# An encoder layer on one core: differences of the weights tied to their place on DVE, bias tables copied in the value passes, masks between sums, turns of late tiles moved in two stages

## The chip, the cores and the metric

The kernel runs on 1 core of one Trainium2 chip. The metric is the device time of one execution in microseconds, the median of several runs. The engines are PE (TensorE, matmuls), PEld (its weight loads), DVE (VectorE), ACT (ScalarE), POOL (GpSimd) and SP, which here only issues DMAs.

## The reference, cut to what matters

```python
# x: (1, 1024, 1024) float32, one layer
h = swiglu(rmsnorm(x, ffn1_pre_g), w_gate1, w_up1, w_down1)      # D_FF = 2816
x = x + 0.5 * rmsnorm(h, ffn1_post_g)
h = rmsnorm(x, mix_pre_g)
q, k, v = split(h @ w_qkv)                                       # 16 heads of 64
o_na  = neighbourhood_attention(q[:8], k[:8], v[:8], na_rel_bias)   # 2-D window, bias, softmax
o_dil = dilated_mixture_attention(q[8:], k[8:], v[8:], t5_rel_bias) # 3 dilated windows, merged
x = x + rmsnorm(concat(rmsnorm(o_na), rmsnorm(o_dil)) @ w_out, mix_post_g)
h = swiglu(rmsnorm(x, ffn2_pre_g), w_gate2, w_up2, w_down2)
x = x + 0.5 * rmsnorm(h, ffn2_post_g)
```

All inputs and outputs are float32.

## The kernel before

**Numbers.** Every operand of a large matmul is split into two parts, `hi` (rounded by an ACT cast) and `lo` (the rest, one DVE subtraction), and a product is three matmuls, hi·hi, hi·lo and lo·hi (`mm3`, lines 317 to 319). Weights go through `split` (ACT line 413, DVE line 414) in the projections, and through `Passes.fetch` (ACT line 673, DVE line 674) in the passes below.

**Strassen's scheme.** The large products are cut into 2 by 2 blocks and done with seven products instead of eight (Winograd's form). On the side of the activations the sums are named A11, A12, A22, S1, S2, S3, S4, on the side of the weights B11, B21, B22, T1, T2, T3, T4, and the pairs are A11·B11, A12·B21, S2·T2, S1·T1, S4·B22, S3·T3, A22·T4. The rows of the activations are 8 tiles of 128. A11 and A12 need only tiles 0 to 3; the others need tiles 4 to 7 too, so those *late tiles* are normalized, transposed on PE and added up (`right_half`, lines 269 to 279) while PE already multiplies with A11 and A12.

**The stages, in order of time.**
- The opening and `PairGemm.ahead` of the first FFN (0 to 85 us): tiles 0 to 3 are normalized, then A11 and A12 products of 9 early blocks of the gate and up weights run while tiles 4 to 7 come in.
- `PairGemm.run` (85 to 470 us): per block five groups of 12 matmuls on PE. For an *early* block (the first 9 of 22; 10 of 22 in the second FFN, all 8 in the query and key projection) their order is S2·T2, then A22 of the block before (in `last`), S1·T1, S3·T1, S4·B22. A later block starts with A11, A22 of the block before, S2, A12, S1, S3, S4. `prepare(b + 1)` hands out the steps for the next block's weights: `direct` (for a later block the split `g`, then three subtractions, lines 502 to 504, which make T1, T2 and T4 from the raw block), `second` (T2's split), `sums` (T1's split) and `rest` (B22's split, and the loads of a raw block two further, lines 407 and 408). The result of S2 is added up in `u` (line 540), of S1 in `v` (line 548), of S3 in `c22` (line 567), of A22 in `c21` (line 575). For the gate, `last` ends with a SiLU on ACT (626) and line 627, and in every second block with four more DVE operations (635 to 638).
- `Passes` of the first FFN's down projection (470 to 689 us): seven passes, one for each product, `pw` split just ahead of use. In its turns `RightSums` makes T1 to T4 of the value weights (loads `tr`, three DVE subtractions at lines 385 to 387 tied behind DVE, one store `tsv`, then the load of the next into the same single buffer), and `masked` adds the mask to the bias tables of 8 heads (POOL line 875, loads and stores of `nb`).
- The value projection's first two passes (689 to 717 us), the query and key projection's `ahead` (717 to 768), the value projection's passes 2 to 6 (768 to 823), the query and key projection's `run` (823 to 950, line 502 among its DVE work). In the first two the late tiles get their residual added (`fin.rest`, line 788), are normalized (squares at line 150 on ACT, `rstd_of` at lines 131 to 143, scaling at line 204) and transposed (`put`).
- Attention (950 to 1200), the output projection, the second FFN (to 1926 us).

**The order.** PE follows the order of the program everywhere. On all other engines a planner puts the instructions in order beforehand, by its own costs and due times: it may put one that it takes to be ready ahead of others that stand earlier in the program. An engine then runs its list strictly in that order, so an instruction that waits holds everything behind it. In the very first stretch (`begin`) DVE and ACT are in the program's order too. `c.behind(f, E)` is the one tool against the planner: what `f` issues on engine `E` is put behind the last instruction that the program had issued on `E` before it.

**Turns.** `plan(n, {i: steps})` fills a list of turns; each unit of matmuls ends with `c.tick()`, which runs one turn. Steps that a turn leaves behind (`put` of a tile: two transposes; pending sums) are run one by one inside the matmul loops (`c.step`). `plan` first flushes what is still open. `spread(steps, 36)` lays a list evenly over 36 turns. In the tables of turns `F` normalizes tiles, `L` loads them, `U` transposes one, `A` adds the residual and normalizes.

**Bias tables.** `c.toeplitz` are eight copies in DRAM (`gab` from `tab`, line 852, POOL's queue, 511 KB each) that lay out the T5 bias for the dilated heads.

Of the kernel before, what the change touches and what calls it, by code (L numbers as in the profile page):

```python
# [391 lines left out]
class PairGemm:  # L392
# [134 lines left out]
    def run(self, final=None):  # L527

        c, nc, sp = self.c, self.c.nc, self.c.sp
        last = None  # L530
        for b in range(self.n):
            w, early = self.w.pop(b), b < self.early
            direct, second, sums, rest = self.prepare(b + 1)
            if early:
                s1 = sp.tile([P, T], F32, tag="s1", name="s1")
                nc.sync.dma_start(s1, self.kept[b])
                a = self.bank()
                self.mm(a, w[T2], 0, S2)
                u2 = sp.tile([P, T], F32, tag="u2", name="u2")
                nc.vector.tensor_add(u2, a, s1)  # L540
                if last:
                    last()
                direct()
                second()
                a = self.bank()
                self.mm(a, w[T1], 0, S1)
                v = sp.tile([P, T], F32, tag="v", name="v")
                nc.vector.tensor_add(v, a, u2)  # L548
            else:
                a = self.bank()  # L550
                self.mm(a, w["g"], 0, A11)
                s1 = self.keep(a, "s1")
                if last:
                    last()
                self.mm(a, w[T2], 0, S2, True)
                u2 = self.keep(a, "u2")
                pb = self.bank()
                self.mm(pb, w["g"], 1, A12)
                self.sink.first(b, pb, False, s1)
                direct()  # L560
                second()
                self.mm(a, w[T1], 0, S1, True)
                v = self.keep(a, "v")
            d = self.bank()
            self.mm(d, w[T1], 1, S3)
            c22 = c.cp.tile([P, T], F32, tag="g2", name="c22", bufs=3)
            nc.vector.tensor_add(c22, d, v)
            sums()
            self.mm(a, w[B22], 0, S4, True)
            self.sink.second(b, a, u2 if early else None)  # L570

            def last(b=b, d=d, w=w, u2=u2, c22=c22, rest=rest):
                self.mm(d, w[B22], 1, A22, True)
                c21 = c.cp.tile([P, T], F32, tag="c", name="c21")
                nc.vector.tensor_add(c21, d, u2)  # L575
                rest()
                self.sink.last(b, c21, c22)
            c.tick()
        if final:
            final()  # L580
        last()
# [657 lines left out]
def layer(tc, a, out):  # L1239
    nc = tc.nc  # L1240
    c = Ctx(tc)
    with ExitStack() as ctx:
# [50 lines left out]
        def plan(n, at):  # L1293

            c.flush()

            def turn(fs):
                return lambda: [f() for f in fs]
            c.todo.extend(turn(at.get(i, ())) for i in range(n))

        def spread(steps, n, skip=0):
            m, n = len(steps), n - skip
            plan(n + skip, {skip + k: steps[m * k // n:m * (k + 1) // n] for k in range(n)})
# [19 lines left out]
        def ffn(which, op, prep, pg, get, turns, sums, more, post, pre, src, dst, begin=None, tables=()):  # L1323
# [57 lines left out]
            ps.take = combine(c, fin.half, rows)  # L1381
            if masks:
                c.bp = pool("bp", 1, m)
            spread(more + masks, 36)
            c.todo[7] = lambda f=c.todo[7]: (f(), c.behind(
                lambda: nc.scalar.activation(fin.gain, fin.gain, AF.Copy, scale=0.5), ACT))
            ps.run(0, 1, 2, 3, 4)
# [61 lines left out]
        with ExitStack() as order:  # L1449
# [25 lines left out]
            def begin(pg):  # L1475
# [92 lines left out]
                for b in range(3):  # L1568
                    if b:
# [5 lines left out]
                order.close()  # L1575
                order.enter_context(ordered())
                return s1
            F = lambda *ts: lambda: op0.norm(ts, [xs[t] for t in ts])
            L, U = (lambda *ts: lambda: load(ts, [nc.gpsimd] * 2)), (lambda t: lambda: op0.put(t))
            op, fin, hs, prep = ffn(1, op0, prep, gate_pairs(1, op0, a["wg1"], a["wu1"], 9), get1,  # L1580
                                    {0: [F(4, 5), L(6, 7)], 1: [U(4)], 2: [F(6, 7), U(5)], 4: [U(6)], 5: [U(7)]},
                                    down_sums(a["wd1"], ts1), value_sums(a["wv"], tsv),
                                    a["ffn1_post_g"], a["mix_pre_g"], x0, x1, begin,
                                    bias_steps(c, *[a[k] for k in ("na_rel_bias", "t5_rel_bias", "onehot", "lncount", "cmask")]))
# [9 lines left out]
            def vearly(p, t, ps):  # L1594
# [4 lines left out]
                else:  # L1599
# [3 lines left out]
            pg = PairGemm(c, op, [(a["wqk"][p], a["wqk"][8 + p]) for p in QK_ORDER], 8, QKPairs(c))  # L1603
            p0 = pg.own = pool("p0", 1, prep, side="right")
            vp.fetch([[p0.tile([P, 2, T], F32R, tag="g" + h, name="pw0" + h) for h in ("hi", "lo")]])
            plan(12, {0: [lambda: fin.scale(4, 4), A(4, 5)], 4: [A(6, 7)], 7: [U(4)], 9: [U(5), lambda: queued(pg.start)],
                      11: [lambda: pg.split_left(0)]})
            vp.run(0, 1, upto=1)
            e.close()
            early_pools(e, 2, 2)  # L1610
            c.qkbufs = 2
            plan(8, {1: [U(6)], 3: [U(7)]})
            pg.ahead()
            c.flush()
            e.close()
# [8 lines left out]
                nc.gpsimd.dma_start(c.v[1][t * P:(t + 1) * P, :], h[:, 1])  # L1624
            vp.take = combine(c, lambda t, g, h: None, vrows)
            nc.sync.dma_start(c.second[:, :, 0], vs1.rearrange("t p x -> p t x"))
            vp.run(2, 3)
            pg.fetch(0)
            pg.fetch(1)
# [9 lines left out]
            def first_bias():  # L1639
                by_residue(nc.gpsimd.tensor_copy, loaded[0][2][:, 0], loaded[0][2][:, 2])  # L1640
            e1 = c.small.tile([P, 1], F32, tag="e1", name="e1", bufs=1)
            plan(8, {**{i: c.toeplitz[2 * i:2 * i + 2] for i in range(4)}, 5: [lambda: queued(load_head)], 7: [lambda: queued(load_head), lambda: queued(first_bias),
                     lambda: c.behind(lambda: nc.scalar.activation(e1, c.ident[:, :1], AF.Exp), ACT)]})
            pg.run()
            w.close()
# [204 lines left out]
```

## Time and profile before

| what | value |
|---|---|
| median of 3 runs | 1929.8 us (1928.88 to 1931.73) |
| the profiled execution | 1927.83 us, its span 1926.0 us |
| PE busy | 1851.6 us, 96% of the span |
| DVE busy | 1325.9 us, 69% |
| ACT busy | 832.0 us, 43% |
| POOL busy | 319.9 us, 17% |
| mean granted clock of PE | 0.988 |

Matmuls overlap each other, and their ends are modelled, so the busy time of PE says only where it had something in flight; what is left, 74.4 us, is time in which it had nothing. "A <- B" in a list of waits reads: the instruction group A waited until B ended; the numbers are the total in us, how often, and the longest. In a timeline a row has the start and the length in us, the engine, the line and the tiles, and in brackets the idle time before it with what ended it. In a table of stretches (windows) the columns are the length, the busy time and instruction count of PE, PEld, DVE, ACT and POOL, then the granted clock of PE, the busy share of the DMA engines, and GB/s. In a list of DMA issues the last number is the median time in us from issue to landing.

### The profile page before, as it was taken

The numbers are of one execution on the slowest core, as the hardware profiler recorded it, in microseconds if no ns is written. First come the engines' busy times: TensorE is split into PE (matmuls) and PEld (weight loads), VectorE is DVE, ScalarE is ACT, GpSimd is POOL, SyncE is SP. The second block draws the span as 40 slices with busy tenths as digits, with TensorE's granted clock in tenths as the row PEclk, the third lists the DMA queues.
The fourth block names the chain that finished last, engine by engine and source line by source line (L and its number), as shares of the span: only waits on it lengthen the run. The fifth ranks groups of instructions, "written<-read, shape, count | busy, mean of one in ns | idle before, by whom it ended". The sixth has DMA issues, their size and how long they took to land.

```text
span 1926.0 us, 25147 instructions
## 1 busy us (share of the span) xinstructions
PE 1851.6 (96%) x8904; PEld 1536.5 (80%) x8904; DVE 1325.9 (69%) x2233; ACT 832.0 (43%) x1491; POOL 319.9 (17%) x504
## 2 busy tenths in 40 slices
PE   7899999999999989998899998999999999999997
PEld 6787888888778867877799997877888888888886
DVE  6777776765565875556677765777788777654557
ACT  7422333333344555223488765455222333344332
POOL 2123211111030122122433100121111111110000
PEclk9999999999999999999999999999999999999999
DMA  7656565547886757556968540575456655476563
GB/s 270 211 169 207 204 225 211 195 164 248 295 306 216 269 187 257 193 178 221 299 224 259 170 142 23 190 280 186 158 192 238 216 193 210 159 267 216 200 227 136
DMA packets 169296, 404.95 MB, mean 210 GB/s; under 512 B 17793, under 2 KB 40225, under 8 KB 167122
## 3 DMA queue, kind: packets, MB, share of 16 engines
q1 hardware_dynamic: 121330, 242.66, 37.9%
q0 software_dynamic: 46832, 158.59, 22.9%
q10 hardware_dynamic: 1008, 2.10, 0.3%
q8 instruction: 70, 1.15, 0.2%
q14 instruction: 56, 0.46, 0.1%
HBM read 277.34 MB, written 130.99 MB: 212 GB/s over the span
## 4 chain that ended last, share of the span: by engine, by line
PE 47%; issue 27%; DMA 9%; DVE 9%; POOL 3%; ACT 3%; SPq 1%; DVEq 0%; POOLq 0%; ACTq 0%
PE mmp L319 9%; PE mmp L317 9%; PE mmp L318 9%; PE accp L318 4%; PE accp L319 4%; PE accp L317 4%; PE po L1072 2%; PE ptp L982 2%; DMA wraw<-in_wqk_dram 2%; PE po L1184 2%; DMA wraw<-in_wu_dram 1%; DVE pw L674 1%; DMA tsv<-tr 1%; PE sp L1051 1%; DVE wlo L414 1%
## 5 line engine op out<-in xcount | busy, mean ns | idle before, releaser
L317 PE MATMUL mmp<-x,whi 128*128 128x512 f32 (+1 forms) x1464 | 581.4, 397 | 19.4 <-DVE v L548 10.9
L319 PE MATMUL mmp<-x,wlo 128*128 128x512 f32 (+1 forms) x1464 | 577.5, 394 | 3.9 <-DVE wlo L414 3.9
L318 PE MATMUL mmp<-x,whi 128*128 128x512 f32 (+1 forms) x1464 | 575.7, 393 | 1.3 <-DVE x L240 0.8
L317 PEld LDWEIGHTS mmp<-x,whi 128*128 128x128 f32 x1464 | 278.2, 190 | 84.7 <-ACT whi L413 10.0
L319 PEld LDWEIGHTS mmp<-x,wlo 128*128 128x128 f32 x1464 | 277.9, 190 | 68.6 <-DVE wlo L414 5.9
L318 PEld LDWEIGHTS mmp<-x,whi 128*128 128x128 f32 x1464 | 278.3, 190 | 62.6 <-DVE x L240 1.1
L674 DVE TENSOR_TENSOR pw<-praw,pw 128x1024 fp32r<-128x1024 f32 (+1 forms) x181 | 199.7, 1148 | 115.7 <-ACT pw L673 115.3
L673 ACT CAST pw<-praw 128x1024 fp32r<-128x1024 f32 (+1 forms) x181 | 168.6, 982 | 208.3 <-PE accp L319 150.3
L318 PE MATMUL accp<-pw 128*128 128x512 f32 x600 | 234.4, 391 | 5.9 <-DVE pw L674 5.6
L317 PE MATMUL accp<-pw 128*128 128x512 f32 x600 | 234.8, 391 | 0.3 <-DVE hb L730 0.2
L319 PE MATMUL accp<-pw 128*128 128x512 f32 x600 | 233.6, 389 | 0.0
L413 ACT CAST whi<-wraw 128x1024 fp32r<-128x1024 f32 x129 | 135.3, 1051 | 219.1 <-PE mmp L318 184.5
L414 DVE TENSOR_TENSOR wlo<-wraw,whi 128x1024 fp32r<-128x1024 f32 x129 | 158.2, 1228 | 19.9 <-ACT whi L413 19.7
L318 PEld LDWEIGHTS accp<-pw 128*128 128x128 f32 x600 | 112.7, 188 | 31.6 <-DVE pw L674 9.0
L317 PEld LDWEIGHTS accp<-pw 128*128 128x128 f32 x600 | 112.7, 188 | 25.1 <-ACT pw L673 1.2
L319 PEld LDWEIGHTS accp<-pw 128*128 128x128 f32 x600 | 112.6, 188 | 23.3
L621 POOL DMA_DIRECT2D g<-sg x44 | 23.9, 544 | 471.1 <-DVE sg L614 296.4
L413 ACT CAST whi<-traw 128x512 fp32r<-128x512 f32 x52 | 32.4, 623 | 152.3 <-DVE traw L503 95.6
L502 DVE TENSOR_TENSOR wraw<-wraw 128x1024 f32<-128x1024 f32 x52 | 63.7, 1225 | 45.4 <-DMA wraw<-in_wqk_dram 26.2
L432 ACT COPY s<-mmp 128x512 f32<-128x512 f32 x52 | 30.6, 588 | 139.4 <-PE mmp L319 136.4
L575 DVE TENSOR_TENSOR c<-mmp,u 128x512 f32<-128x512 f32 x52 | 35.9, 690 | 76.9 <-PE mmp L319 76.8
L1184 PE MATMUL po<-vs,pt 128*128 128x128 f32 x352 | 50.3, 276 | 2.0 <-ACT pt L984 1.7
(278 smaller groups left out, 2761.1 us busy)
## 6 DMA issues: line engine op xcount, KB each, us to landing
praw<-g SPq DMA_DIRECT2D x70, 512.0 KB, 6.0
wraw<-in_wg_dram SPq DMA_DIRECT2D x44, 512.0 KB, 4.2
wraw<-in_wu_dram SPq DMA_DIRECT2D x44, 512.0 KB, 6.2
tr<-in_wd_dram SPq DMA_DIRECT2D x44, 512.0 KB, 6.5
g<-sg POOLq DMA_DIRECT2D x88, 256.0 KB, 4.1
ts<-tr POOLq DMA_DIRECT2D x22, 1024.0 KB, 4.8
praw<-ts SPq DMA_DIRECT2D x88, 256.0 KB, 4.3
praw<-in_wd_dram SPq DMA_DIRECT2D x66, 256.0 KB, 4.9
```

The source lines that it names most:

```text
L317: nc.tensor.matmul(out, ahi, bhi, start=start, stop=False, skip_group_check=go_on)
L318: nc.tensor.matmul(out, ahi, blo, start=False, stop=False, skip_group_check=go_on)
L319: nc.tensor.matmul(out, alo, bhi, start=False, stop=stop, skip_group_check=go_on)
L413: nc.scalar.copy(hi, raw)
L414: nc.vector.tensor_sub(lo, raw, hi.bitcast(F32))
L502: nc.vector.tensor_sub(r[:, 0:2], r[:, 1:3], r[:, 0:2])
L575: nc.vector.tensor_add(c21, d, u2)
L673: nc.scalar.copy(hi, raw[:, :m])
L674: nc.vector.tensor_sub(lo, raw[:, :m], hi.bitcast(F32))
L982: nc.tensor.transpose(ps[:, j, :], src[:, j * P:(j + 1) * P], c.ident)
L1072: nc.tensor.matmul(po[:, un * 2 + j], pt[:, 2 * j + t, :], rhs, start=t == 0, stop=t == 1)
L1184: nc.tensor.matmul(po[0][:, u], pt[0][:, j, :], vs[:, k0 + j, :], start=j == 0, stop=j == n - 1)
```

## The change

Five edits in one:
1. In `PairGemm.run`, `direct()` becomes `c.behind(direct, DVE)` for early and for later blocks: the DVE instructions of `direct` are put behind the last DVE instruction that the program issued before.
2. The nine mask steps no longer stand behind the five steps of the value weights' sums (one load, four sums), but two by two between them, over the same 36 turns.
3. In the opening the squares of `F` are put behind ACT's last instruction; tiles 6 and 7 are normalized at turn 1 instead of 2 and transposed at turns 5 and 6 instead of 4 and 5.
4. Around the value projection's first passes, `A(6, 7)` moves from turn 4 to turn 10, `U(4)` from 7 to 8, `pg.start` from 9 to 8, `split_left(0)` from 11 to 10, and `U(5)`, `U(6)`, `U(7)` go to turns 0, 3, 5 of the query and key projection's `ahead` (from turn 9 before it, and 1, 3 in it).
5. The eight copies of the bias table move from turns 0 to 3 of the query and key projection's `run` (two a turn) to every second turn, 0 to 14, of the value passes 2 to 6.

```diff
@@ PairGemm.run @@
                 if last:
                     last()
-                direct()
+                c.behind(direct, DVE)
                 second()
...
                 self.sink.first(b, pb, False, s1)
-                direct()
+                c.behind(direct, DVE)
                 second()
@@ ffn @@
-            spread(more + masks, 36)
+            steps = more[:1]
+            for i, f in enumerate(more[1:]):
+                steps += masks[2 * i:2 * i + 2] + [f]
+            spread(steps + masks[2 * len(more[1:]):], 36)
@@ layer, first FFN @@
-            F = lambda *ts: lambda: op0.norm(ts, [xs[t] for t in ts])
+            F = lambda *ts: lambda: c.behind(lambda: op0.norm(ts, [xs[t] for t in ts]), ACT)
...
-                                    {0: [F(4, 5), L(6, 7)], 1: [U(4)], 2: [F(6, 7), U(5)], 4: [U(6)], 5: [U(7)]},
+                                    {0: [F(4, 5), L(6, 7)], 1: [U(4), F(6, 7)], 2: [U(5)], 5: [U(6)], 6: [U(7)]},
@@ layer, value, query and key projection @@
-            plan(12, {0: [lambda: fin.scale(4, 4), A(4, 5)], 4: [A(6, 7)], 7: [U(4)], 9: [U(5), lambda: queued(pg.start)],
-                      11: [lambda: pg.split_left(0)]})
+            plan(12, {0: [lambda: fin.scale(4, 4), A(4, 5)], 8: [U(4), lambda: queued(pg.start)],
+                      10: [lambda: pg.split_left(0), A(6, 7)]})
...
-            plan(8, {1: [U(6)], 3: [U(7)]})
+            plan(8, {0: [U(5)], 3: [U(6)], 5: [U(7)]})
...
+            plan(20, {2 * i: [f] for i, f in enumerate(c.toeplitz)})
             vp.run(2, 3)
...
-            plan(8, {**{i: c.toeplitz[2 * i:2 * i + 2] for i in range(4)}, 5: [lambda: queued(load_head)], 7: [...
+            plan(8, {5: [lambda: queued(load_head)], 7: [...
```

More of the change, by code (lines that the diff above doesn't have):

```diff
@@ L1641, in layer @@
             e1 = c.small.tile([P, 1], F32, tag="e1", name="e1", bufs=1)
-            plan(8, {**{i: c.toeplitz[2 * i:2 * i + 2] for i in range(4)}, 5: [lambda: queued(load_head)], 7: [lambda: queued(load_head), lambda: queued(first_bias),
+            plan(8, {5: [lambda: queued(load_head)], 7: [lambda: queued(load_head), lambda: queued(first_bias),
                      lambda: c.behind(lambda: nc.scalar.activation(e1, c.ident[:, :1], AF.Exp), ACT)]})
```

## The prediction

> **What bounds the kernel now.** I read the page's first lines, then the list of waits of PE, then the granted clock and the DVE timeline of each place that the list names.
>
> ```profile
> span 1926.0 us, 25147 instructions
> PE 1851.6 (96%) x8904; PEld 1536.5 (80%) x8904; DVE 1325.9 (69%) x2233; ACT 832.0 (43%) x1491; POOL 319.9 (17%) x504
> ...
> PE mmp L317 <- DVE v L548: 10.9, 7, 2.8
> PE accp L318 <- DVE pw L674: 6.0, 7, 1.7
> PE trp L157 <- DVE x L204: 5.5, 1, 5.5
> PE trp L157 <- DVE xn L204: 4.9, 1, 4.9
> ...
> PE mmp L319 <- DVE wlo L414: 3.9, 3, 3.1
> ...
> PE mmp L317 <- ACT x L238: 2.6, 1, 2.6
> ```
>
> PE sets the end: 1926.0 - 1851.6 = 74.4 us are all that better timing alone can win there. The waits shown are 34 us of it, and all but the last are on DVE, which is busy only 69% of the span: what is wanted is done too late, not too slowly. Beside the waits stands the clock.
>
> ```profile
> 20.00:60.00 40.00, 31.02 (x149) 24.66 (x148) 32.43 (x64) 25.73 (x44) 11.88 (x22) 0.94 0.79 283
> 690.00:730.00 40.00, 31.38 (x131) 24.95 (x130) 30.69 (x66) 20.36 (x34) 11.17 (x20) 0.91 0.63 217
> 838.00:950.00 112.00, 98.85 (x429) 79.94 (x427) 71.57 (x96) 38.48 (x51) 32.41 (x46) 0.98 0.79 252
> 870.00:885.00 15.00, 12.59 (x50) 9.98 (x49) 11.67 (x15) 6.96 (x8) 5.37 (x8) 0.89 0.65 183
> 160.00:200.00 40.00, 39.80 (x172) 31.52 (x172) 31.33 (x43) 9.35 (x11) 12.28 (x22) 1.00 0.53 169
> ```
>
> What the column behind POOL's count (0.94, 0.91, 0.98) lacks of 1, times the length, is the clock lost in three stages: 2.4, 3.6 and 2.2 us. It goes where waits are, and is 1.00 in a gate stage without them (last row).
>
> **The change part by part.** The sum is made against the profiled execution (1927.8 us, span 1926.0 and 1.8 around it), which lies 2.0 under the median shown. An edit at a time:
>
> *D, the query and key run (edits 1 and 5).* Its order and its loads:
>
> ```profile
> PE mmp L317 <- DVE v L548: 10.7, 6, 2.8
> ...
> DVE wraw L502 <- DMA wraw<-in_wqk_dram: 24.4, 5, 6.6
> 851.46 1.23 DVE L502 TENSOR_TENSOR wraw<-wraw 128x1024 f32<-128x1024 f32 x1 [4.08 <-DMA wraw<-in_wqk_dram]
> 860.82 0.68 DVE L548 TENSOR_TENSOR v<-mmp,u 128x512 f32<-128x512 f32 x1
> 859.17 10.88 DMA wraw<-in_wqk_dram
> wraw<-in_wqk_dram SPq DMA_DIRECT2D x16, 512.0 KB, 6.3
> ```
>
> The planner has put `direct` (L502) ahead of `k` and `u`, although it stands behind `last` in the program. L502 waits for its raw block, DVE stands still (24.4 us in five blocks), everything behind it is late, and `v` holds PE: 10.7 of the 10.9 us lie between 838 and 950. Tied, `direct` comes behind `last`, where the block (it landed at 851.46, and is then wanted from about 859) is there; and without the copies, during which such loads take 10.88 us against a median of 6.3, it lands earlier. What is late next is T2 for the next S2. Behind the last line 931, `direct` to T2's `lo` takes 1.23 + 0.68 + 0.69 + 0.62 + 0.68 = 3.9 us (rows in E), while PE has S1, S3 and S4 to do, 8.2 us from the end of A22: nothing waits if line 931 ends within 4.3 us of it. An addition, three or four ACT operations and two subtractions of 0.6 to 1.1 us come first, some of them side by side, so I put it at 4.7: 0.4 us a block stay, 3 over eight. Gain 10.7 - 3 + 1.6 of the clock (870 to 885: 0.11 of 15) = 9, bounds 2 (`direct` only moved to another wait) and 12.9 (10.7 + 2.2).
>
> *E, the gate runs (edit 1).* PE does not wait there today, and this is the price. Rows of a block whose `last` ends with four more operations:
>
> ```profile
> 171.28 1.05 ACT L413 CAST whi<-wraw 128x1024 fp32r<-128x1024 f32 x1 [1.16 <-PE mmp L318]
> 169.50 0.62 ACT L413 CAST whi<-traw 128x512 fp32r<-128x512 f32 x1 [5.43 <-DVE traw L503]
> 166.96 1.23 DVE L502 TENSOR_TENSOR wraw<-wraw 128x1024 f32<-128x1024 f32 x1 [1.64 <-DMA wraw<-in_wu_dram]
> 171.11 0.68 DVE L414 TENSOR_TENSOR wlo<-traw,whi 128x512 fp32r<-128x512 f32 x1
> 176.88 0.69 DVE L638 TENSOR_TENSOR sg<-sg 128x512 f32<-128x512 f32 x1
> 850.53 0.39 PE L317 MATMUL mmp<-x,whi 128*128 128x512 f32 x1
> 853.25 0.39 PE L317 MATMUL mmp<-x,whi 128*128 128x512 f32 x1
> ```
>
> A group of 12 matmuls takes 853.25 - 850.53 = 2.72 us. The cast at 171.28 starts when A22 ends; S1, S3 and S4 follow, so the next S2 wants T2 at 171.28 + 8.2 = 179.4. Before, T2 was ready at 171.8, because `direct` had run at 167. Tied behind L638 (end 177.6), L502 and L503 (0.68, as line 414's half) end at 179.4, the cast at 180.1, T2's `lo` at 180.8, which S2's third matmul wants at 179.9: 0.7 to 0.9 us late, and 1.8 if T1's cast (1.05) goes first on ACT. I take 1.4. It hits blocks 3, 5, 7 of the first FFN and 3, 5, 7, 9 of the second: +10. In the other early blocks `direct` follows L627 and can push `v`, but by no more than one L502 of 1.23 less some 0.5 of slack: 0.7 each, of which I take nothing, as the planner would have to choose it. Later blocks start with A11 and A22, 5.4 us more: nothing; the S2 and A12 groups cover `direct` there. Bounds 0 (if the planner finds gaps for it) and 7 x 1.8 + 8 x 0.7 = 18.
>
> *A, the opening (edit 3).*
>
> ```profile
> 25.64 1.06 ACT L150 ACTIVATE xn<-x 128x1024 f32<-128x1024 f32 x1 [1.01 <-DMA x<-in_x_dram]
> 49.56 0.17 DVE L133 TENSOR_SCALAR v<-ss 128x2 f32<-128x2 f32 x1
> 56.58 2.48 DVE L204 SCALAR_TENSOR_TENSOR xn<-x,y,gain 128x1024 f32<-128x1024 f32 x2
> ```
>
> Two squares, for tiles 4 and 5, stand in front of the casts (L238) that PE waits for 2.6 us; the first waits 1.01 for its tile and takes 1.06. Behind ACT's last instruction they let the casts go some 1.9 us earlier, and tile 4, squared later, takes some of that back: 1.5. The wait of 4.9 us is tile 6: its chain of small operations runs from 49.56, between the sums of tile 5, to the scaling at 56.58; a turn sooner, it starts before these. A turn later is two groups, 5.4 us, which covers 4.9. But DVE is full there (32.43 of 40), so I take 4 of it. With 1 of the 2.4 us of clock: 1.5 + 4 + 1 = 6.5, bounds -2 (tile 7's sums, now in front of the last blocks' splits, hold one of them up by two operations of 0.69 and a little) and 10 (2.6 + 4.9 + 2.4).
>
> *B, sums and masks (edit 2).*
>
> ```profile
> DVE tr L385 <- DMA tr<-in_wv_dram: 20.2, 4, 7.3
> tr<-in_wv_dram SPq DMA_DIRECT2D x8, 512.0 KB, 4.5
> tsv<-tr POOLq DMA_DIRECT2D x4, 1024.0 KB, 8.1
> ```
>
> One round of the single buffer takes 4.5 + 8.1 + 2.6 (1.23 + 2 x 0.69) = 15 us. Four sums over turns 5 to 12 come faster and stop DVE for 20.2 us; PE loses most of its 6.0 us on `pw` behind them, and some of it because a load that waits for the buffer holds the `praw` loads behind it in SP's queue. With two masks between them they come every seven or eight turns, 16 to 20 us. The hold on SP's queue stays as long as it was; POOL, which adds the masks, is 17% busy and nobody in this stage waits for it. Gain 3, half, bounds -1 (masks and sums share the DMA engines) and 6.
>
> *C, late tiles around the value projection (edit 4).*
>
> ```profile
> 692.42 4.87 DVE L788 SCALAR_TENSOR_TENSOR x<-hb,y,x 128x1024 f32<-128x1024 f32 x4
> 702.55 2.48 DVE L204 SCALAR_TENSOR_TENSOR x<-x,y,gain 128x1024 f32<-128x1024 f32 x2
> 722.10 2.35 DVE L414 TENSOR_TENSOR wlo<-graw,whi 128x1024 fp32r<-128x1024 f32 x2
> ```
>
> PE waits 5.5 us for tile 4's scaling, which follows the residuals of four tiles and their squares. With tiles 6 and 7 at turn 10 half of the 4.87 us can come out from under it, of which I take 1.5, since the squares on ACT stay; and U(4) one turn later asks for it 2.7 later (one group): 1.3 of the wait stay, 4.2 go. The second wait, 3.1 us, is the split of the second weight block behind tile 5's sums; these go into the next stage, but tiles 6 and 7 bring 2 x 2.48 back. I take 1.3 of it, and 2 of the 3.6 us of clock: 7.5, bounds -3 (tile 7, two blocks later, late for S2) and 12.
>
> *F, eight copies in the value passes (edit 5).*
>
> ```profile
> DVE wraw L502 <- DMA wraw<-in_wqk_dram: 1.8, 2, 1.1
> ```
>
> These passes load four raw halves of the projection, and `begin`'s L502 stands for them in DVE's list ahead of `pw` splits. From the slow loads above (10.88 for 6.3) each may be up to 4.6 us later; PE has one or two splits in hand. I take +2, bounds 0 and 5. By the Trainium skill ("DMA: Bandwidth & Descriptors", Issuing engines are not separate DMA queues), DMAs of all engines share the same 16 DMA engines and interleave, so that POOL's copies only change whom they slow; by that rule F would be nearer +4.6 and the sum 2.6 less good. The trace agrees for the stage they leave (10.88); for the one they enter it shows nothing yet.
>
> Sum: -9 + 10 - 6.5 - 3 - 7.5 + 2 = **-14 us**. 1927.8 becomes 1913.8, and the median 1929.8 becomes 1916.
>
> **The rivals.**
> 1. *The ties cost nothing in the gates*, because T2's subtractions find DVE idle in the planner's list. For it: DVE idles before A22 ends (160 to 200: 31 of 40 busy). Against: L638's place. E = 0: -24, 1906.
> 2. *The waits only move.* DVE is as full around 50 and 700 as before, and the same work is late somewhere else. A -2, B -1, C -2, D -7, E +10, F +2 = 0: 1930. For it: 30.69 of 40 in C.
> 3. *Slower: T2 starves S2 in the gate runs.* 18 us of E, and each of seven waits grows to 2.4 us or so and takes a slow stretch of 1.6 with it, as one in 870 to 885 did: 18 + 11 = 29, against 26 - 2 elsewhere: +5, 1935. It decides once E passes 24, or 1.6 us on each of the 15 blocks concerned. By the Trainium skill ("TensorE: Matmul & The Clock Gate", Part 1: The HAM clock gate) the clock halves after an idle window of about 3.4 us, so waits under 2 us cost none; by that rule this rival would end at -6, 1924. The trace disagrees in part: its 0.89 in 870 to 885 stands where no wait exceeded 2.8 us.
> 4. *The tie changes nothing where it should*: with the loads late, `direct` waits at its new place too, and D is 3 at most. -8: 1922. Against: the load that ended at 851.46 would be wanted some 7 us later.
>
> **How the numbers follow.** Forecast 0.35, rivals 0.23, 0.20, 0.12, 0.10. About 0.2% (3.9 us, 1926 to 1934) is what a measurement can tell from no change. Faster: the forecast, the first and fourth rival and a third of the second, 0.76; same 0.13; slower, most of the third and a little of the second, 0.11. The range 1901 to 1932 goes from the first rival less 5 us (A or C at its bound) to the second plus 2; outside lie a tenth above and some 0.06 below.
>
> **What would show it.** D: L502 without DMA waits between 838 and 950, PE's wait on `v` under 3 us. E: PE waits on `wlo`/`whi` from `traw` at every second early gate block, 0.7 to 1.8 us each. A: no wait on `xn` L204; squares behind L432. B: the wait of L385 under 8 us, PE on `pw` under 3. C: at most 1.3 us on L204. F: L502's wait between 768 and 823 over 1.8 us, with a wait on `pw`. Wrong if PE waits over 24 us in the gate runs, or if its waits in A and C come back under other names.

## The result, and the profile after

The changed kernel takes 1928.0 us (median of 20 runs, 1923.1 to 1935.1), the kernel before 1927.3 in the same comparison (20 runs, 1921.4 to 1933.1): a ratio of 1.0003 with a 95% interval of 0.9992 to 1.0014. No change can be told. Forecast were 1916.

The profiled execution of the changed kernel has a span of 1922.6 us. Its busy times from the page, and the head of its list of waits of PE (engine and line, what it waited for, us in total, times, longest):

```profile
span 1922.6 us, 25127 instructions
...
PE 1848.9 (96%) x8904; PEld 1532.5 (80%) x8904; DVE 1330.8 (69%) x2233; ACT 831.8 (43%) x1491; POOL 320.3 (17%) x504
```

```profile
PE mmp L317 <- ACT whi L413: 11.9, 8, 2.3
PE mmp L319 <- DVE wlo L414: 8.6, 9, 1.2
PE accp L317 <- ACT pw L673: 5.2, 3, 3.0
...
PE accp L318 <- DVE pw L674: 4.2, 6, 0.9
...
PE trp L157 <- DVE xn L204: 3.1, 1, 3.1
...
PE mmp L317 <- DVE v L548: 2.4, 4, 0.6
```

PE stands 1922.6 - 1848.9 = 73.7 us, against 74.4 before. The list has been turned over all the same: `v` fell from 10.9 to 2.4, the wait of 5.5 for tile 4 of the value projection is 0.8, tile 6's 4.9 in the opening are gone, and in their place stand `whi` and `wlo` (4.4 and 3.9 before, 20.5 together now), the cast `pw` of line 673, and a new wait on `xn`.

Where this happens is read by stages. Each begins with its first group of matmuls in PE's timeline and ends with the first of the next; "passes" are the first FFN's passes with the value passes 0 and 1, "blocks ahead" the first query and key blocks, "later value passes" the passes 2 to 6. The forecast is split by the terms of the prediction's sum (E by 1.4 us a block, three and four of them).

| stage | before | after | difference | forecast |
|---|---|---|---|---|
| opening and first gate run | 462.9 | 467.5 | +4.6 | -2.3 (A, three of E) |
| passes | 254.0 | 243.5 | -10.5 | -10.5 (B, C), with the next |
| blocks ahead | 51.1 | 47.1 | -4.0 | |
| later value passes | 55.4 | 63.8 | +8.4 | +2 (F) |
| query and key run | 122.7 | 112.8 | -9.9 | -9 (D) |
| attention and its output projection | 321.0 | 318.7 | -2.3 | 0 |
| second gate run | 438.4 | 448.5 | +10.1 | +5.6 (four of E) |
| second FFN's passes | 220.6 | 220.7 | +0.1 | 0 |

24.4 us were won in three stages, and the profile gives back 23.1 in three others. The windows that answer to those of before (length, busy us by engine, then PEclk, DMA share, GB/s) show both sides:

```profile
20.00:60.00 40.00, 35.53 (x167) 28.88 (x166) 32.09 (x65) 27.52 (x46) 12.47 (x24) 0.91 0.75 265
690.00:730.00 40.00, 37.32 (x168) 29.54 (x167) 33.12 (x64) 25.74 (x42) 13.43 (x24) 1.00 0.71 241
823.00:935.00 112.00, 109.59 (x481) 89.22 (x480) 79.92 (x104) 40.55 (x52) 28.14 (x39) 1.00 0.66 217
160.00:200.00 40.00, 38.85 (x168) 30.72 (x167) 31.24 (x42) 10.51 (x13) 12.06 (x22) 1.00 0.55 176
```

The passes and the query and key run are at full clock now; the gate run's window, in which PE was busy 39.80 of 40 us, has lost 0.95. The waits of DVE that the prediction worked with (DVE and its line, us, times, longest) went as it said:

```profile
DVE wraw L502 <- DMA wraw<-in_wqk_dram: 5.6, 1, 5.6
...
DVE tr L385 <- DMA tr<-in_wv_dram: 1.5, 1, 1.5
```

The value sums' 20.2 us are 1.5. Of 26 us of L502 one wait is left, but it is in a new place, the later value passes. There is no row on `in_wu_dram` any more in this view of the whole span: tied, `direct` never stands at the gate's loads. That looks like a gain, and the next view, DVE around a block of the gate run whose `last` ends with L638, shows what it costs:

```profile
150.50 0.69 DVE L638 TENSOR_TENSOR sg<-sg 128x512 f32<-128x512 f32 x1
151.10 1.22 DVE L502 TENSOR_TENSOR wraw<-wraw 128x1024 f32<-128x1024 f32 x1
152.24 0.69 DVE L567 TENSOR_TENSOR c<-mmp,v 128x512 f32<-128x512 f32 x1
152.84 0.68 DVE L503 TENSOR_TENSOR traw<-wraw 128x512 f32<-128x512 f32 x1
153.56 1.22 DVE L414 TENSOR_TENSOR wlo<-wraw,whi 128x1024 fp32r<-128x1024 f32 x1
154.70 0.69 DVE L504 TENSOR_TENSOR wraw<-wraw,traw 128x512 f32<-128x512 f32 x1
155.30 0.69 DVE L414 TENSOR_TENSOR wlo<-traw,whi 128x512 fp32r<-128x512 f32 x1
```

L502 follows L638 as foreseen. But between it and T2's `lo` (155.30) stand L567, T1's `lo` (1.22, at 153.56) and L504. PE, whose timeline around it reads

```profile
154.57 0.40 PE L318 MATMUL mmp<-x,whi 128*128 128x512 f32 x1
156.04 0.50 PE L319 MATMUL mmp<-x,wlo 128*128 128x512 f32 x1 [1.08 <-DVE wlo L414]
```

waits 1.08 us for that `lo`. Here and in the block at 185 us the matmuls of the bias table (L843, 1.02 us) happen to fill the wait for T2's cast that comes before it; the block at 123 and the four of the second gate run lose both, 1.0 to 1.2 us each.

### The profile page after: what moved, and what is told of

It reads as the page before. It is cut to its first block, busy times and chain, and to the rows that moved or that the text cites. A ratio compares the mean times of both kernels' runs of the same rounds, so it can differ in the third digit from the quotient of the medians.

```text
span 1922.6 us, 25127 instructions
## 1 busy us (share of the span) xinstructions
PE 1848.9 (96%) x8904; PEld 1532.5 (80%) x8904; DVE 1330.8 (69%) x2233; ACT 831.8 (43%) x1491; POOL 320.3 (17%) x504
## 4 chain that ended last, share of the span: by engine, by line
issue 44%; PE 35%; DMA 7%; POOL 6%; DVE 5%; ACT 3%; SPq 0%; POOLq 0%; DVEq 0%; ACTq 0%
PE accp L318 5%; PE accp L319 5%; PE accp L317 5%; PE mmp L319 4%; PE mmp L318 4%; PE mmp L317 4%; PE po L1072 2%; PE ptp L982 2%; POOL g L640 2%; PE po L1184 2%; PE sp L1051 1%; DMA tr<-in_wd_dram 1%; DMA ts<-tr 1%; PE sp L1168 1%; PE trp L157 1%
## 5 line engine op out<-in xcount | busy, mean ns | idle before, releaser
L414 DVE TENSOR_TENSOR wlo<-wraw,whi 128x1024 fp32r<-128x1024 f32 x129 | 157.9, 1225 | 24.4 <-ACT whi L413 24.0
L502 DVE TENSOR_TENSOR wraw<-wraw 128x1024 f32<-128x1024 f32 x52 | 63.5, 1221 | 6.4 <-DMA wraw<-in_wqk_dram 5.6
```

What stands on the lines that cost most here:

```text
L414: nc.vector.tensor_sub(lo, raw, hi.bitcast(F32))
L502: nc.vector.tensor_sub(r[:, 0:2], r[:, 1:3], r[:, 0:2])
```

## The experiments

All ratios are to the kernel before, run beside them on the same chip, with 95% intervals. Stages and waits are from the profiled execution of each.

**1. The ties in the query and key run alone.** The changed kernel, with

```diff
-                c.behind(direct, DVE)
+                c.behind(direct, DVE) if isinstance(self.sink, QKPairs) else direct()
```

> The changed kernel, with the tie of direct kept in the query and key run alone. Theory (the gate runs pay for the tie, the rest of the ledger stands): the waits on whi and wlo at every second early gate block (12.6 us with those at 123, 155, 185 and four after 1358) go, the first FFN's gate run is some 4.5 us shorter, the second's 10: about 1913 us, 0.992 of the kernel before. Rival (waits only move: DVE is late somewhere else as soon as PE is not): within 4 us of the kernel before.

Measured: 1908.9 us, 0.9895 [0.9880, 0.9911]; the changed kernel has 1.0003. The tie in the gate runs costs 0.0108, 21 us. The profile (span 1908.6) takes 6.2 us off the first stage and 9.1 off the second gate run, 15.3, and leaves all others within 1 us. Its list of waits of PE for the first gate run holds one row:

```profile
PE mmp L317 <- DVE v L548: 0.2, 1, 0.2
```

against 3.2 on `wlo` and 1.0 on `whi` in the changed kernel. So E is 15 us in one pair of executions and about 21 in the medians, where +10 was forecast. A part of the distance between the two is the profiled execution of the changed kernel, which lies at 1924.4 with the 1.8 us around its span, 3.7 under that kernel's median, while that of this experiment (1910.4) lies 1.5 over its own; experiment 2 shows another.

**2. The tie alone.** The kernel before with edit 1 and nothing else.

> The kernel before, with edit 1 alone (ties in early and later blocks, copies where they were). Theory: both gate runs together lose 14 us, the query and key run gains 7 to 10 although the copies still run in it, since the tie alone takes L502 out of DVE's way: 4 to 8 us slower, 1932 to 1935. Rival (the copies cause the waits of the query and key run, the tie does little): the run between 823 and 946 stays near 122 us, 14 us slower in all, 1941.

Measured: 1950.4 us, 1.0112 [1.0094, 1.0130], 22 us slower: far above the expectation, and above its rival too. The first stage is 9.4 us longer than before, the second gate run 15.8, and the query and key run, where the tie was to win 9, is 2.2 us *longer*. PE's waits in that run:

```profile
PE mmp L317 <- ACT whi L413: 8.3, 3, 2.9
PE mmp L317 <- DVE v L548: 1.2, 2, 0.7
PE mmp L319 <- DVE wlo L414: 1.1, 3, 0.7
```

The 10.7 us on `v` are 1.2; 8.3 us on T2's cast stand in their place. A tied `direct` hardly holds `v` up any more, but it comes behind a late L931, and T2 is late. DVE before one of the three waits, which ends at 905.04:

```profile
899.42 0.69 DVE L567 TENSOR_TENSOR c<-mmp,v 128x512 f32<-128x512 f32 x1 [2.03 <-PE mmp L319]
900.03 0.68 DVE L931 TENSOR_TENSOR qk<-qk 128x512 fp32r<-128x512 f32 x1
900.62 1.07 DVE L931 TENSOR_TENSOR qk<-c,qk 128x512 fp32r<-128x512 f32 x1
901.61 1.22 DVE L502 TENSOR_TENSOR wraw<-wraw 128x1024 f32<-128x1024 f32 x1
...
903.34 0.69 DVE L503 TENSOR_TENSOR traw<-wraw 128x512 f32<-128x512 f32 x1
```

D's wait moved instead of going. L502 does not wait for a load once in this run now (24.4 us before). It is late because the planner has put L567, which waits 2.03 us for PE, ahead of L931, and the tied `direct` comes behind that. In the changed kernel L567 stands behind L931, L502 and L503.

The gate runs' surplus over the changed kernel (4.8 us in the first stage, 5.7 in the second gate run) is mostly clock. In 100 to 200 us both kernels wait for the same 3.2 us on `wlo` and 1.0 on `whi`. The windows around two of these waits, first in the changed kernel:

```profile
122.00:132.00 10.00, 7.90 (x34) 5.86 (x33) 6.51 (x10) 2.45 (x3) 4.42 (x9) 1.00 0.73 246
153.00:163.00 10.00, 8.85 (x35) 6.13 (x35) 6.79 (x10) 2.73 (x4) 2.84 (x6) 1.00 0.60 219
```

and then with the tie alone:

```profile
122.00:132.00 10.00, 7.90 (x27) 5.76 (x26) 7.31 (x11) 1.67 (x2) 4.04 (x8) 0.84 0.75 252
153.00:163.00 10.00, 8.85 (x29) 5.85 (x28) 7.93 (x11) 1.66 (x2) 3.29 (x7) 0.83 0.72 239
```

PE is busy for equally long, 7.90 and 8.85, but 27 and 29 matmuls are recorded in place of 34 and 35. The clock lacks 0.16 and 0.17 of 10 us, 1.6 and 1.7 us. In PE's timeline a matmul behind the second wait takes 0.68 and 0.63 us, where it takes 0.39 otherwise:

```profile
159.30 0.68 PE L319 MATMUL mmp<-x,wlo 128*128 128x512 f32 x1 [1.07 <-DVE wlo L414]
159.78 0.63 PE L317 MATMUL mmp<-x,whi 128*128 128x512 f32 x1
```

Waits of the same length took a stretch of slow clock in one execution and none in the other.

**3. The copies back in the query and key run.** The changed kernel with its ties, and with the eight copies where they were before.

```diff
-            plan(20, {2 * i: [f] for i, f in enumerate(c.toeplitz)})
...
-            plan(8, {5: [lambda: queued(load_head)], 7: [...
+            plan(8, {**{i: c.toeplitz[2 * i:2 * i + 2] for i in range(4)}, 5: [lambda: queued(load_head)], 7: [...
```

> The changed kernel with the eight copies back in turns 0 to 3 of the query and key run. Theory (the copies hold L502 in the value passes, the tie protects the run): the stretch of passes 2 to 6 falls from 64.0 us by 5 to 6 and keeps some 2 us over the 55.5 of before, which come from tile 7's later turns; the query and key run stays within 2 us of 112.8: about 1923 us. Rival (passes 2 to 6 are longer because of the later turns of tiles 5 to 7 alone): that stretch stays at 64, and the time is that of the changed kernel or more.

Measured: 1937.3 us, 1.0054 [1.0036, 1.0071]. The query and key run goes from 112.8 back to 125.1, with the same 8.3 us on `whi` as in experiment 2, and the later value passes from 63.8 to 59.1. So the tie did not shorten that run; the absence of the copies did. The expectation, that the tie protects it (about 1923 us), was wrong. But late loads are not the way here: as in experiment 2, L502 waits for none in this run, and each of the three waits on `whi` follows an L567 that waits for PE and stands ahead of the last L931 and the tied `direct`. With the tie in, the copies' place changed the planner's order. The profiled execution (1928.9) is the fastest of eleven, 8.4 under their median.

**4. The late tiles' turns alone.** The kernel before with edit 4.

> The kernel before, with edit 4 alone (turns of the late tiles around the value projection). Theory: the waits on line 204 (5.5 us), on the second weight split (3.1) and two slow stretches of 1.7 go, 8 to 11 us by the end of the query and key projection's ahead, and passes 2 to 6 give 2 to 3 back because their first weights are split late: 6 to 8 us faster, about 1921. Rival (waits only move): under 3 us.

Measured: 1924.6 us, 0.9979 [0.9965, 0.9992], 4 us faster where 6 to 8 were expected. Passes -4.3, blocks ahead -4.0, later value passes +4.5. From the last of the passes to the end of the later value passes PE waited 5.5 us on L204, 3.1 on `wlo` and 0.4 on `pw` before. With edit 4 its list for this stretch has only:

```profile
PE accp L317 <- ACT pw L673: 2.7, 2, 1.5
PE accp L318 <- DVE pw L674: 2.1, 3, 0.8
```

9.0 us of waits became 4.8 on the splits of the next weights, part of them at the start of value pass 2, whose first splits now come only when the query and key blocks are done with tile 7.

**5. The masks between the sums alone.** The kernel before with edit 2.

> Kernel before with edit 2 alone (masks put between the sums of the value weights). Theory: the sums' waits for the single buffer (20.2 us of DVE before, 1.5 in the changed kernel) go with this edit and with no other, and PE's 5.6 us on pw in the first FFN's passes fall below 3; the passes with value passes 0 and 1 become 5 to 7 us shorter (254.0 to 247..249), the whole 1921 to 1923. Rival (the masks share the DMA engines with the sums, what goes comes back under another name): that stretch moves by less than 2, the whole 1926 to 1928.

Measured: 1921.8 us, 0.9970 [0.9958, 0.9981], as expected for the whole; the passes became 250.0, a little less short than the 247 to 249 expected. Its wait of L385 for the value weights:

```profile
DVE tr L385 <- DMA tr<-in_wv_dram: 1.4, 1, 1.4
```

The 20.2 us go with this edit and, by experiment 4, where they stay at 20.5, not with the turns; PE's 5.6 us on `pw` in the passes fall to 1.5. The passes give 4.0 us. The blocks ahead are 2.2 shorter (48.8), but not by this edit: experiments 2, 6 and 7, which change nothing there, have 48.7 too. 1.7 of it is a slow stretch of clock at 724 us that only the profile of the kernel before has.

**6. The opening alone.** The kernel before with edit 3.

> Kernel before with edit 3 alone (squares of tiles 4 to 7 behind ACT's last instruction, turns of tiles 6 and 7 moved). Theory after the changed kernel's profile: PE's 4.9 us on xn of L204 (tile 6) become some 3 us on the same line for tile 4, the 2.6 us on L238 go, and a wait of 2 us for T2's cast behind the late squares comes in near 80 us, with a slow clock stretch moved rather than removed: the stage 0 to 2 us shorter, the whole 1926 to 1928. Rival, the prediction's own: -6.5, 1921.

Measured: 1925.4 us, 0.9984 [0.9972, 0.9996], some 3 us. The first stage of the profile is 0.9 us longer than before; its waits:

```profile
PE trp L157 <- DVE xn L204: 3.1, 1, 3.1
PE mmp L317 <- ACT whi L413: 2.2, 1, 2.2
...
PE mmp L317 <- ACT x L238: 0.7, 1, 0.7
```

These are the changed kernel's to a tenth, so both new waits of its opening are this edit's: 4.9 (tile 6) went and 3.1 (tile 4) came, 2.6 on L238 became 0.7, and 2.2 on `whi` are new. All of PE's waits from 20 to 95 us are 7.5 us here and 9.0 before. The stage is longer all the same, because the clock lost more: it is 0.91 from 20 to 60 us and 0.86 from 80 to 92, against 0.94 and 1.00 before.

**7. The copies moved, and nothing else.** The kernel before with edit 5.

> Kernel before with the second half of edit 5 alone: the eight table copies go into value passes 2 to 6, no tie, nothing else. Theory (the copies' share of the DMA engines holds the query/key run up, not the place of direct): with direct untied the run becomes 113 to 115 (122.7 before), value passes 2 to 6 become 59 to 61 (55.4), the whole 1921 to 1923. Rival (tie and copies are both needed, as the prediction had it): the run stays at 119 or more, the whole 1928 to 1931.

Measured: 1922.6 us, 0.9970 [0.9960, 0.9980]. With `direct` untied, the query and key run takes 109.0 us, 13.7 less than before and 3.8 less than in the changed kernel, and PE has no wait in it at all. The raw blocks that it loads, before (all in that run; the last column is us from issue to landing):

```profile
wraw<-in_wqk_dram SPq DMA_DIRECT2D x10, 512.0 KB, 7.1
gab<-tab POOLq DMA_DIRECT2D x8, 511.0 KB, 7.9
```

and with the copies moved:

```profile
wraw<-in_wqk_dram SPq DMA_DIRECT2D x10, 512.0 KB, 5.0
```

`direct` has kept its place in DVE's list for the first blocks, in front of `k` and `u`; the block that waited 4.08 us before, at 851.46, now reads

```profile
856.60 1.23 DVE L502 TENSOR_TENSOR wraw<-wraw 128x1024 f32<-128x1024 f32 x1 [0.84 <-DMA wraw<-in_wqk_dram]
```

and `v` is in time. All of L502's waits in this run are 4.5 us, for 24.4. From the fourth block on the order of DVE's instructions differs as well, so not every microsecond is the loads' alone.

The later value passes pay for it: 63.7 us, 8.4 more. PE's waits there, L502's, and the loads of raw blocks:

```profile
PE accp L317 <- ACT pw L673: 3.2, 1, 3.2
PE accp L318 <- DVE pw L674: 2.0, 1, 2.0
PE accp L317 <- DVE hb L724: 1.0, 1, 1.0
```

```profile
DVE wraw L502 <- DMA wraw<-in_wqk_dram: 7.2, 1, 7.2
```

```profile
wraw<-in_wqk_dram SPq DMA_DIRECT2D x6, 512.0 KB, 10.1
```

The same loads take 6.1 us in this stage before. One of them is 7.2 us late for L502, and 6.2 us of PE follow; from 794 to 806 us the clock is 0.72, 3.4 us more.

**8. No tie at all.** The changed kernel with `direct()` as before: edits 2 to 5.

> Changed kernel without any tie (edits 2 to 5 left). Theory: the tie is worth nothing in the query/key run once the copies are out of it; that run stays within 2 us of 112.8 and the whole is 1908 to 1911, as in the kernel with the tie there alone (1908.9). Rival: without the tie PE's wait on v of L548 comes back, 4 to 8 us, and the whole is 1913 to 1918.

Measured: 1906.9 us, 0.9894 [0.9877, 0.9912], not to be told from experiment 1 by time. In the profile the query and key run is 109.0 us, without a wait of PE, against 112.6 with the tie there. Its window:

```profile
817.00:926.00 109.00, 109.00 (x483) 90.27 (x482) 78.45 (x100) 40.36 (x51) 28.02 (x39) 1.00 0.68 224
```

PE is busy for all of it. Where the tie was to win, it loses 3.6 us; the rival, that the wait on `v` comes back without it, falls.

**9. The copies in the first gate run.** Experiment 8, with the copies one a turn from the gate run's eighth turn on, behind the writing of the table.

```diff
-            plan(20, {2 * i: [f] for i, f in enumerate(c.toeplitz)})
...
             if tables:
                 c.bp = pool("bp", 1, w)
+                for i, f in enumerate(c.toeplitz):
+                    tables.setdefault(7 + i, []).append(f)
```

> Changed kernel without any tie, and with the eight copies in the first FFN's gate run (one a turn from the eighth on, after the table is written) instead of the value passes. Theory (the copies cost where PE's weights are only just in time, and nothing where DVE and the loads are well ahead): value passes 2 to 6 fall from 65.1 to 59 to 60 (what the late turns of tiles 5 to 7 cost stays), the query/key run stays at 109 to 110, the gate run stays within 1 us; the whole 1900 to 1903 (1906.9 without this move). Rival (the copies slow the gate run's weight loads as they did those of the query/key run): that run gains 4 us or more, the whole 1905 or more.

Measured: 1905.3 us, 0.9886 [0.9865, 0.9906]: a little slower than expected, and not to be told from experiment 8. By stages it is as the theory has it: later value passes 61.0 in place of 65.1, the query and key run 109.0, the first stage 461.7 in place of 460.5 without one wait of PE in the gate run. What is lost again lies in stages that the edit does not touch (opening, passes and attention: 1.2, 1.2 and 1.1). The loads in the gate run from 187 to 320 us, with the copies among them:

```profile
wraw<-in_wu_dram SPq DMA_DIRECT2D x8, 512.0 KB, 6.2
gab<-tab POOLq DMA_DIRECT2D x7, 511.0 KB, 4.4
```

A copy here takes 4.4 us, not 7.9, and the weights' loads 6.2, where experiment 8, without the copies, has 6.0 for the same loads in these 133 us.

**10. Tiles 6 and 7 a turn earlier.** Experiment 9 with

```diff
-            plan(8, {0: [U(5)], 3: [U(6)], 5: [U(7)]})
+            plan(8, {0: [U(5)], 2: [U(6)], 4: [U(7)]})
```

> The kernel above, with tiles 6 and 7 put at turns 2 and 4 of the first query/key blocks in place of 3 and 5. Theory (tile 7's late turn ends the buffers of the stage late, so that value pass 2's first splits are late): PE's waits on pw at the start of value passes 2 to 6 (2.6 us in the kernel above's parent) fall below 1, the passes become 57 to 58, the whole 1898 to 1901. Rival (turn 4 makes tile 7's chain delay the query/key blocks' splits, as before the change): the first query/key blocks grow by 1 to 3 us and nothing is won.

Measured: 1899.9 us (five runs, 1899.3 to 1904.9), 0.9863 [0.9839, 0.9887], 26 us faster than the kernel before. One of these five times, taken beside those of experiment 9, lies within that experiment's range (1901.4 to 1909.5); the others lie below it. The later value passes take 57.7 us and the blocks ahead 47.0, as with the later turns. PE's waits in the later value passes:

```profile
PE accp L318 <- DVE pw L674: 2.4, 3, 1.2
```

The waits at the start of value pass 2 (3.2 us in experiment 9) are gone, and with them 1.7 us of slow clock at 760. The 2.4 us that are left lie in the middle of the stage, where experiment 9 has 0.6, so a part of the 3.2 did come back.

**11 and 12. The two halves of the opening.** Experiment 10 with the squares untied again (the first two lines of the diff), and with edit 3 undone altogether (all four).

```diff
-            F = lambda *ts: lambda: c.behind(lambda: op0.norm(ts, [xs[t] for t in ts]), ACT)
+            F = lambda *ts: lambda: op0.norm(ts, [xs[t] for t in ts])
...
-                                    {0: [F(4, 5), L(6, 7)], 1: [U(4), F(6, 7)], 2: [U(5)], 5: [U(6)], 6: [U(7)]},
+                                    {0: [F(4, 5), L(6, 7)], 1: [U(4)], 2: [F(6, 7), U(5)], 4: [U(6)], 5: [U(7)]},
```

> The fastest kernel so far (no tie of direct, copies in the gate run, tiles 6 and 7 at turns 2 and 4; 1899.9) with the squares of tiles 4 to 7 untied again, edit 3's turns kept. Theory: the two halves of edit 3 each make one of the opening's two new waits; untied, tile 4's 3.3 us on xn of L204 go and the 2.6 us on L238 of the kernel before come back, and the 2.2 us on whi at 79 stay; the whole 1898 to 1902. Rival: the tie is what edit 3 is worth, tile 6's 4.9 us come back without it, the whole 1903 to 1906.

> The same kernel with edit 3 undone altogether (the opening of the kernel before). Theory: tile 6's 4.9 us and the 2.6 us on L238 come back, tile 4's 3.3 and the 2.2 at 79 go: 2.0 us of waits more and a clock stretch more or less, the whole 1901 to 1904. Rival (edit 3 is worth nothing, its waits only move): within 1.5 us of 1899.9. Rival, the prediction's A: 6.5 more, 1906.

Measured: untied 1901.0 us, 0.9864 [0.9850, 0.9879]; undone 1902.2, 0.9871 [0.9854, 0.9887]. Neither is to be told from experiment 10. The first stage is 461.4 with edit 3, 460.8 untied and 463.6 undone. With the squares untied PE's first two waits in the opening are

```profile
PE mmp L317 <- ACT x L238: 2.8, 1, 2.8
PE mmp L317 <- ACT whi L413: 2.2, 1, 2.2
```

and with edit 3 undone 4.9 us on `xn` of L204 (tile 6) and 2.3 on L238.

So the tie of the squares only puts tile 4's 3.3 us in the place of 2.8 on L238, and the turns put 2.2 us on `whi` in the place of tile 6's 4.9. What edit 3 is worth stays between nothing and 3 us: 2 us less of PE's waits from 20 to 95 us (9.0 in experiment 12, 7.1 in 10), 2.2 by the first stage here, 3 (1 to 5) by experiment 6's ratio, but 0.9 the other way by experiment 6's first stage. By these profiles it comes from its turns; the times of 10, 11 and 12 can't tell.

## Why the prediction was wrong

The signs and the places came out almost everywhere; four sizes and one cause did not. By the table the profiles miss the forecast by some 11 us: 6.9 and 4.5 in the two gate stages (A and E) and 6.4 in the later value passes (F, and a bill of C's), less 4.0 in the stages of B and C, 0.9 in D and 2.3 in attention.

**E, mis-sized: +10 forecast, 15 in the profiles and about 21 in the medians (experiment 1).** Blocks and mechanism were right: three blocks of the first and four of the second gate run, T2 behind L638. The step that failed took 1.4 us a block, between 0.7 to 0.9 for T2's `lo` and 1.8 with T1's cast first on ACT. What happened is the second case and one more: on DVE, T1's `lo` (1.22 us) goes ahead of T2's as well, so that PE waits first for T2's cast, then for its `lo`. The seven blocks wait for 4.2 us in the first run and 8.8 in the second, and would wait for 15 if the table's matmuls did not fill two gaps. With a slow stretch of clock in the second run (1.7) that is 15 of the profile. The rest is clock that comes and goes between executions: the gate runs of experiment 2 have seven slow stretches that cost 1.7 us each, those of the changed kernel two. The granted clocks of all executions bear this out: 0.9898 on average for the changed kernel (20 executions) and 0.9918 for experiment 1 (4). What they lack of 1, times the spans, differs by 4 us: by this estimate 4 of the some 20 us between the two kernels are clock, and 15 to 16 would be there at full clock. This was the third rival's way: T2 starved S2, and slow clock followed. It was to decide from 24 us, and reached 15 to 21.

**D, right by 1 us and for the wrong reason.** The step that failed is the one that gave 9 us to the tie and the loads together, with the place of `direct` as the cause. Experiments 7 and 8 show the run at 109.0 without the tie, 2 and 3 at 125 with the tie and the copies in. The copies in that run were the cause, worth 13.7: the raw blocks landed after 7.1 us with them and 5.0 without. With the tie they cost 12.3 (experiment 3), by the order on DVE and no longer by late loads. The tie takes back 3.6 to 3.8. The signs that were named for D, no wait of L502 for loads and under 3 us on `v`, hold in experiment 2 too, where the run got longer: they can't tell a gain from a wait that has moved to T2. The row that told it stood in the prediction (a load of 10.88 us beside a median of 6.3), but was used only as a help to the tie.

**F, mis-sized: +2 forecast.** The chain was the one described: raw blocks late, L502 waiting in front of the `pw` splits. But the loads (six in this stage, not four) went from 6.1 us to 11.1 in the changed kernel, 5.0 later where up to 4.6 was said, L502 waited 5.6 us, longer than the one or two splits that PE has in hand, and a slow stretch of clock came on top (PEclk 0.83 in 784 to 794). Alone, the move costs 8.4 us in this stage (experiment 7), above the upper bound of 5. In the changed kernel it costs 4.7, since with the copies out the stage still takes 59.1 (experiment 3): the other 3.7 of the 8.4 are edit 4's. The Trainium skill ("DMA: Bandwidth & Descriptors", Issuing engines are not separate DMA queues) says that DMAs run on the same 16 DMA engines and interleave, whichever engine started them. The runs agree: POOL's copies make SP's loads later, 11.1 us for 6.1. The +4.6 that the prediction drew from this was nearer than its +2. What neither said is that it matters where: in the gate run the same copies slow nobody that PE waits for (experiment 9).

**C, the gains right, a bill left out.** Passes and blocks ahead went down by 8.3 us with edit 4 alone, as the 7.5 said, though some 2 of it stand in the blocks ahead of experiments 2, 6 and 7 as well. The bound of -3, "tile 7, two blocks later, late for S2", named the right tile and the wrong victim: not S2, but the first splits of value pass 2. Edit 4 alone costs 4.5 us there, and one turn earlier for two tiles takes 3.3 of it back (61.0 to 57.7, experiment 10), half of that by a slow stretch less.

**B, better than said.** 6 us in place of 3 by experiment 5's ratio, 4.0 by its passes: the buffer's waits were 4.1 of PE's 5.6 us on `pw`, not half.

**A, mis-sized: -6.5 forecast, some -2 by the waits.** "A turn later covers 4.9" was right for tile 6. "Tile 4, squared later, takes some of that back" was sized as 0.4 of 1.9 us and is a wait of 3.1; and the later turns made T2's cast 2.2 us late near 80 us, which no step had looked for. Nor did the 1 us of clock come: 20 to 60 us stood at 0.94 and stands at 0.91.

Of the rivals, the second (the waits only move: 1930) is nearest to the total, but not by its terms: B and C won more than was forecast, and the ties and the copies' new place took it back. The fourth, that the tie changes nothing where it should, is nearly what experiments 2 and 8 show, though not by its reason: `direct` does not wait for loads at its new place. The single edits add up: from the ratios, 22 for the ties, -6 for the masks, -3 for the opening, -4 for the turns, -6 for the copies are +3, and together they measured +1 with an interval of 2 us either way. Without the ties the sum is -19, and experiment 8 measured -20. By stages they do not add up: edits 4 and 5 lengthen the later value passes by 4.5 and 8.4 alone, and by 8.4 together.

Of the 2.3 us by which attention and its output projection, which no edit touches, became shorter, 1.7 are a slow stretch of clock at 1188 us that the changed kernel's profile lacks; those of experiments 2, 4, 6, 8 and 9 have it. Each kernel has one profile, so single stages can't be read to better than 2 us or so. For whole executions the granted clock is on record: 0.9875 on average for the kernel before (28 executions beside experiments 5 to 8), 0.9898 for the changed one (20) and 0.9920 for experiment 10 (5). What they lack of 1, times the span, is 24, 20 and 15 us. By this estimate the changed kernel would be some 4 us slower than the one before at full clock. What stays open is why a wait costs such a stretch in one execution and none in the next.

## What to carry to other kernels

Where an engine waits for a load in front of urgent work, ask first what slows the load: eight copies taken out of the stage were worth 13.7 us, the reordering that was to live with them less than nothing. A tie that fixes the order for one consumer holds for every block that runs through that line; its price is read block by block, with all that the planner can then put ahead of the tied work on each engine. And background transfers belong in a stage by the slack of what they delay, not by its DMA share: the gate run had room at 0.6, the value passes had none at 0.55.

## What was not expected of the hardware

The clock falls after waits much shorter than was assumed, and not always. In experiment 2 a block with waits of 1.0 and 1.1 us, and one with a single wait of 1.07 behind the table's small matmuls, were each followed by a slow stretch (0.84 and 0.83 in 10 us); in the changed kernel, with waits of equal length at the same places, none was (1.00 and 1.00). The rule that the prediction cites from the Trainium skill ("TensorE: Matmul & The Clock Gate", Part 1: The HAM clock gate), that it takes an idle window of about 3.4 us, would have given full clock in both.

A copy of 511 KB from DRAM to DRAM landed after 4.4 us in one stage and 7.9 in another, and beside it loads of 512 KB took 6.2 us (6.0 without it) in the one and 7.1 (5.0 without it) in the other; in the later value passes it was 10.1 against 6.1. The DMA share over a stage of the kernel before (0.55 to 0.72) does not tell these apart.
